# A two-layer encoder on one core: layer 0's attention and output projection issued from an instruction list

## The chip, the cores and the metric

The kernel runs on one core of a Trainium2 chip. A core has a matrix engine (TensorE, PE in the rows; its weight loads are PEld), three engines for elementwise work (VectorE is DVE, ScalarE is ACT, GpSimd is POOL) and a queue engine, SyncE (SP), that issues the loads and stores of weights and activations. Each engine works through its own list of instructions in order and waits at semaphores for the others. The metric is the device time of one execution in microseconds (us); the number quoted for a kernel is the median of several.

## The reference

Two groups of tokens, one prompt of 256 and one sample of 512, each with 16 meta tokens in front, go through the same two layers in fp32. Layer 0 is multi-head latent attention, layer 1 a windowed attention with sinks; each is followed by a squared-ReLU MLP, and each of the four sublayers by a residual and a layer norm. What the change touches is layer 0's attention, cut to its core:

```python
def mla_attend(qn, qr, kn, kr, v):
    s = einsum('bqhd,bkhd->bhqk', qn, kn) + einsum('bqhr,bkr->bhqk', qr, kr)
    p = softmax(s * 96 ** -0.5)
    return einsum('bhqk,bkhd->bqhd', p, v)

c = x @ w_in                                   # 1024 -> 768 + 256 + 32
cq, ckv = rms_norm(c[:768]), rms_norm(c[768:1024])
kr = apply_rope(c[1024:])                      # one for all 16 heads
qn, qr = split(cq @ w_uq)                      # 64 + 32 a head
qr = apply_rope(qr)
kn, v = split(ckv @ w_ukv)                     # 64 + 64 a head
h = layer_norm(4 ** 0.25 * h + mla_attend(...) @ w_o)
```

## The kernel before, in words

There are 800 token columns: `s=0` is the prompt (272), `s=1` the sample (528). Activations lie with features on partitions. Every fp32 product is made of three matmuls in a reduced fp32 form (`mm3`, L440 to L443: high x high, high x low, low x high), so each operand is kept as a high part (a cast on ScalarE) and a low part (a subtraction on VectorE); L458 does both for activations, L314 and L315 for weights.

The stages run one after another: input projection (tile `in`), attention of layer 0, its output projection (tile `o`) with the first half of the layer norm beside it, the MLP, attention of layer 1, the second MLP. For layer 0's attention the 16 heads go in eight pairs `p`, each for `s=0` and then `s=1`. The query columns of a group are cut in chunks of about 100: three for `s=0`, where one chunk does both heads of the pair, five for `s=1`, each head apart. For one chunk (`soft_items`, L737):

- TensorE makes the scores in a PSUM tile `s` (six matmuls; two such tiles exist).
- VectorE takes the row maximum (L766, L773) and scales it; ScalarE takes the exponential into the tile `p`, with its row sums (L768, L776); VectorE inverts these (L769, L777).
- The probabilities are multiplied by the inverse. The 16 meta columns and some more go into a small tile `pk` on VectorE (L743), the 256 or 512 others are scaled in place on GpSimd (L744), for each head.
- TensorE transposes them four blocks at a time (tile `t`, L808) and ScalarE copies the result to `pt` (L814); after all chunks of a unit come the product with the values (`av`, L829) and with the meta values (L837).

Between these steps lies the work that fills TensorE: projections to qn, qr, kn and v for the next pair (`fill_items`, L720). `vmz` and `pks` are small tiles whose unused part must be zero; they are set at L629, in the pool `ap0`, which takes memory that the input's activations `x` held before.

What sets the order here is the framework's scheduler. The code is written in program order, with priorities (`ATT_PRIORITY` for scores and products with the values, 0 for transposes, `LN_PRIORITY` for the layer norm), and the scheduler puts single instructions of each engine into a line by its own estimates. Weights come through the class `Weights`, which loads them in a fixed sequence. `EARLY = 4` of the 16 output tiles are begun for the first column half while the last pair's softmax runs (`early_out`, L901).

Everything later, from the MLP of layer 0 on, is made another way already: by the class `Plan` (L90). There code adds tasks with an engine, an estimated cost, what they read and write, and the buffers they need. TensorE's order is the order in which its tasks are added; the other engines' tasks are placed by a list scheduler (`forward`), which picks by due times worked out backwards and lets buffers rotate in the order in which they are freed; then all instructions are issued in that order, each engine's line as planned.

Of the kernel before, what the change touches and what calls it, by code (L numbers as in the profile page):

```python
# [14 lines left out]
ALU = mybir.AluOpType  # L15
# [44 lines left out]
EARLY = 4  # L60
# [4 lines left out]

SCALE_AHEAD = 3
ATT_PRIORITY, LN_PRIORITY = 30, 300


# [20 lines left out]
class Plan:  # L90
# [8 lines left out]
    def __init__(self, bufs, own):  # L99
        self.bufs, self.own, self.tasks, self.last = bufs, own, [], {}  # L100
        self.given = {tag: [] for tag in bufs}
        self.busy = {}
        self.turns = {tag: [] for tag in bufs}
# [46 lines left out]
    def forward(self, deps, after, late):  # L150
# [13 lines left out]
        def start(i):  # L164
# [3 lines left out]
            for h in held:  # L168
                if id(h) not in at:
                    k = turns[h.tag].index(h)  # L170
                    if len(slots[h.tag]) <= k or k and h.tag not in self.own:
                        return None
                    t = max(t, slots[h.tag][0][0])
# [179 lines left out]
def tile_encoder(ctx: ExitStack, tc: tile.TileContext, ins: dict, y):  # L353
# [31 lines left out]
    def ps_t(name):  # L385
        return bank("t", name)

# [30 lines left out]
    for g in range(4):  # L418
        use(("qr", g), ins["w_qr"][g], 768)
        use(("kv", g), ins["w_kv"][g])  # L420
        use(("qn", 2 * g), ins["w_qn"][2 * g], 768)
        use(("qn", 2 * g + 1), ins["w_qn"][2 * g + 1], 768)
    for hf in range(2):
        for o in range(8):
            use(("o0", hf, o), ins["w_o0"][o])
    for layer in range(2):
        w1 = ins[f"w1_{layer}"]
        if layer == 1:
            for j in UP_FIRST[:2]:
                use(("up", j), None, where="given")  # L430
            for i in range(4):
                use(("dn", 7, i), ins["w2c_1"][i], where="held" if i == 3 else "last")
        else:
            for j in UP_FIRST[:2]:
                use(("up", j), w1[j])
            for i in range(3):
                use(("dn", 7, i), None, where="given")
# [44 lines left out]
    def ln_fm(tp, z, ssum, n, gi, bi, hi, lo, tag, pieces=None, behind=None):  # L482

        pm = ps_l(f"lnm{tag}")
        marks = {"pm": nc.tensor.matmul(pm[:, :n], part, ssum, start=True, stop=True).ins}
        vs = [tp.tile([P, HALF], F32, tag=f"lnv{i}", name=f"lnv{tag}{i}")[:, :n] for i in range(2)]
        for o in range(8):
            f = V.tensor_tensor(z[:, o], z[:, o], pm[:, :n], ALU.subtract)
            if behind is not None:
                after(f.ins, behind["los"][min(7, o + 1)])  # L490
            if o < 2:
                S.activation(vs[o], z[:, o], AF.Square)
            else:
                sq = tp.tile([P, HALF], F32, tag="lnsq", name=f"lnsq{tag}_{o}", bufs=4)
                S.activation(sq[:, :n], z[:, o], AF.Square)
                f = (G if o in POOL_SQUARES and tag != "b0" else V).tensor_tensor(vs[o % 2], vs[o % 2], sq[:, :n], ALU.add)
        marks["va"] = f.ins
        rs = rstd_bcast(tp, vs, n, D, eps_ln, f"ln{tag}", marks)
        for o in range(8):
            f = V.tensor_tensor(z[:, o], z[:, o], rs, ALU.mult)  # L500
            if o >= SCALE_AHEAD:
                after(f.ins, marks["los"][o - SCALE_AHEAD])
            for a, b, d in pieces or [(0, n, 0)]:
                f = S.activation(z[:, o, d : d + b - a], z[:, o, a:b], AF.Identity, bias=gb[:, bi, o : o + 1], scale=gb[:, gi, o : o + 1])
                if o > 0:
                    after(f.ins, marks["hi"])
            marks["hi"], marks["lo"] = split(hi[:, o], lo[:, o], z[:, o, : d + b - a])
            marks.setdefault("los", []).append(marks["lo"])
        return marks


# [6 lines left out]
    acc = hp.tile([P, 2, 8, HALF], F32, tag="acc", name="acc")  # L518
    att = ExitStack()
# [71 lines left out]
    psum_phase(s=2, t=2, w=2)  # L591
# [19 lines left out]
    for s in (1, 0):  # L611
# [4 lines left out]
    def krope(s):  # L616
        for ka, kb in ((272, 400), (400, 800)) if s == 1 else ((0, 272),):
            for e in range(2):
                rows = slice(ROPE[e], ROPE[e] + 32)
                c = slice(ka - 272 * s, kb - 272 * s)  # L620
                split(K[s][e][0][rows, c], K[s][e][1][rows, c], kr[rows, ka // HALF, ka % HALF : (kb - 1) % HALF + 1])

# [3 lines left out]
    vmz = [ap.tile([96, 3, 256], F32, tag=f"vm{i}", name=f"vm{i}") for i in range(2)]  # L626
    pks = [[ap.tile([106, 96], F32, tag=f"pk{i}{e}", name=f"pk{i}{e}") for e in range(2)] for i in range(3)]
    for t in vmz + sum(pks, []):
        G.memset(t, 0.0)  # L629
    wkv, wq, V_ = {}, {}, {}  # L630

    early = []

    def ps_p(name):
        tag = early.pop(0) if early else "w"
        return ps_s(name)[:, 0] if tag == "s" else bank(tag, name)
# [4 lines left out]
    def rope_items(g):  # L641
        def piece(s, a, b):
            if s == 0:
                wq["r"] = W.get(("qr", g), 0)
# [302 lines left out]
    for f in late:  # L947
        f()
# [1279 lines left out]
```

## Time and profile before

| | us |
|---|---|
| median of three runs | 1814.65 (1810.26 to 1816.73) |
| the profiled execution | 1813.73 |
| its span in the trace | 1811.9 |
| PE busy, weight loads | 1769.5, 1635.5 |
| DVE, ACT, POOL busy | 1344.1, 1013.8, 784.9 |

The profiled execution is one run of the program; the span is what lies between its first and last record. The input projection ends at 87.3 us; the first scores come at 100.36, the first early output tile at 381.0, the last product with the values ends at 429.2, and the last output tile at 485.5, where the MLP begins. The mean clock that TensorE was granted is 0.992 of full speed.

### The profile page before, as it was taken

The numbers are of one execution on the slowest core, as the hardware profiler recorded it, in microseconds if no ns is written. First come the engines' busy times: TensorE is split into PE (matmuls) and PEld (weight loads), VectorE is DVE, ScalarE is ACT, GpSimd is POOL, SyncE is SP. The second block draws the span as 40 slices with busy tenths as digits, with TensorE's granted clock in tenths as the row PEclk, the third lists the DMA queues.
The fourth block names the chain that finished last, engine by engine and source line by source line (L and its number), as shares of the span: only waits on it lengthen the run. The fifth ranks groups of instructions, "written<-read, shape, count | busy, mean of one in ns | idle before, by whom it ended". The sixth has DMA issues, their size and how long they took to land.

```text
span 1811.9 us, 28961 instructions
## 1 busy us (share of the span) xinstructions
PE 1769.5 (98%) x10808; PEld 1635.5 (90%) x10808; DVE 1344.1 (74%) x2553; ACT 1013.8 (56%) x2141; POOL 784.9 (43%) x617
## 2 busy tenths in 40 slices
PE   9989999999999999999999899999999999999997
PEld 9989889878999999999999898778989888988995
DVE  5478777775876787787786777876875787778777
ACT  5357766773664456445544536775574456545652
POOL 0046655653244456445533133332233566455623
PEclk9999999999999999999999899999999999999998
DMA  5111001103321121221222222011311221222122
GB/s 196 47 42 31 19 22 34 38 29 125 105 82 47 70 70 47 94 70 47 71 82 89 72 70 68 22 60 59 116 47 59 70 70 49 92 70 70 52 89 93
DMA packets 38444, 121.70 MB, mean 67 GB/s; under 512 B 4640, under 2 KB 9376, under 8 KB 38176
## 3 DMA queue, kind: packets, MB, share of 16 engines
q1 hardware_dynamic: 38304, 119.85, 19.8%
q8 instruction: 85, 1.39, 0.3%
q14 instruction: 55, 0.45, 0.1%
HBM read 116.69 MB, written 3.15 MB: 66 GB/s over the span
## 4 chain that ended last, share of the span: by engine, by line
PE 75%; DVE 16%; ACT 5%; issue 2%; POOL 1%; DMA 1%; DVEq 0%; SPq 0%; ACTq 0%; POOLq 0%
PE w L441 14%; PE w L442 14%; PE w L443 14%; PE wb L441 4%; PE wb L442 4%; PE wb L443 4%; DVE h L1099 2%; DVE wsp0d L1057 2%; PE wb L1904 1%; PE in L441 1%; PE in L442 1%; PE in L443 1%; DVE acc L1364 1%; PE wb L1804 1%; PE wb L1886 1%
## 5 line engine op out<-in xcount | busy, mean ns | idle before, releaser
L744 POOL TENSOR_SCALAR p<-p,rs 106x512 f32<-106x512 f32 (+3 forms) x128 | 184.6, 1451 | 136.4 <-DVE pk L743 66.2
L1364 DVE TENSOR_TENSOR acc<-acc,w 128x400 f32<-128x400 f32 (+1 forms) x306 | 177.0, 617 | 21.3 <-PE w L443 18.9
L1099 DVE TENSOR_TENSOR h<-sq,h 128x384 fp32r<-128x384 f32 (+1 forms) x165 | 139.4, 860 | 23.8 <-ACT h L1097 23.6
L441 PE MATMUL w<-h,wsp0d 128*128 128x400 f32 x336 | 116.1, 346 | 1.1 <-DVE acc L1364 1.1
L442 PE MATMUL w<-h,wsp0d 128*128 128x400 f32 x336 | 116.0, 345 | 0.0
L443 PE MATMUL w<-h,wsp0d 128*128 128x400 f32 x336 | 115.6, 344 | 0.0
L441 PE MATMUL w<-wsp1d,h 128*128 128x512 f32 x252 | 100.1, 397 | 5.6 <-DVE acc L1364 5.6
L1105 POOL TENSOR_TENSOR sq<-sq,sq 128x400 f32<-128x400 f32 (+1 forms) x56 | 74.9, 1338 | 69.6 <-DVE h L1099 60.7
L443 PE MATMUL w<-wsp1d,h 128*128 128x512 f32 x252 | 100.2, 398 | 0.2
L442 PE MATMUL w<-wsp1d,h 128*128 128x512 f32 x252 | 99.9, 396 | 0.0
L1097 ACT CAST h<-sq 128x384 fp32r<-128x384 f32 (+1 forms) x165 | 84.6, 519 | 25.6 <-POOL sq L1105 23.9
L1070 POOL TENSOR_TENSOR wraw0d<-wraw0d,wraw0d 128x512 f32<-128x512 f32 x48 | 69.6, 1468 | 41.2 <-DMA wraw0d<-in_w2b_dram 29.1
L768 ACT ACTIVATE p<-s,nm,rq 106x528 f32<-106x528 f32 (+1 forms) x80 | 63.5, 794 | 42.4 <-DVE nm L767 36.0
L1278 DVE TENSOR_TENSOR sq<-sq,w 128x400 f32<-128x400 f32 (+1 forms) x69 | 38.5, 560 | 56.6 <-PE w L443 56.4
L1051 ACT CAST wsp0d<-wraw0d 128x1024 fp32r<-128x1024 f32 x42 | 43.3, 1051 | 57.7 <-POOL wraw0d L1070 45.9
L766 DVE TENSOR_REDUCE nm<-s 106x1 f32<-106x528 f32 (+1 forms) x80 | 55.8, 700 | 19.9 <-PE s L443 19.0
L1057 DVE TENSOR_TENSOR wsp0d<-wraw0d,wsp0d 128x1024 fp32r<-128x1024 f32 x42 | 63.4, 1510 | 7.0 <-ACT wsp0d L1051 7.0
L1070 POOL TENSOR_TENSOR wraw1d<-wraw1d,wraw1d 128x512 f32<-128x512 f32 x36 | 53.3, 1498 | 31.8 <-DMA wraw1d<-in_w2b_dram 14.4
L315 DVE TENSOR_TENSOR wsp<-wraw,wsp 128x1024 fp32r<-128x1024 f32 (+2 forms) x52 | 55.5, 1076 | 15.1 <-ACT wsp L314 14.8
L441 PE MATMUL s<-k,q 128*106 128x264 f32 (+5 forms) x208 | 62.3, 300 | 4.3 <-ACT p L776 3.2
L441 PEld LDWEIGHTS w<-h,wsp0d 128*128 128x128 f32 x336 | 63.1, 188 | 3.0 <-DVE acc L1364 2.8
L441 PEld LDWEIGHTS w<-wsp1d,h 128*128 128x128 f32 x252 | 47.3, 188 | 18.4 <-ACT wsp1d L1051 8.0
(1444 smaller groups left out, 6409.0 us busy)
## 6 DMA issues: line engine op xcount, KB each, us to landing
wraw0d<-in_w2b_dram SPq DMA_DIRECT2D x24, 512.0 KB, 3.2
wraw1d<-in_w2b_dram SPq DMA_DIRECT2D x18, 512.0 KB, 4.2
wraw<-in_w_o_dram SPq DMA_DIRECT2D x16, 512.0 KB, 3.4
wrawo<-in_w_o_dram SPq DMA_DIRECT2D x16, 512.0 KB, 3.3
wrawq<-in_w_q_dram SPq DMA_DIRECT2D x8, 512.0 KB, 3.3
wraw<-in_w_in_dram SPq DMA_DIRECT2D x6, 512.0 KB, 4.6
wraw<-in_w_qn_dram SPq DMA_DIRECT2D x8, 384.0 KB, 3.0
wx1d<-in_w2b_dram SPq DMA_DIRECT2D x6, 512.0 KB, 3.2
```

Source lines behind the costliest of these rows:

```text
L441: nc.tensor.matmul(out, lh, rh, start=start, stop=False, **kw)
L442: nc.tensor.matmul(out, lh, rl, start=False, stop=False, **kw)
L443: nc.tensor.matmul(out, ll, rh, start=False, stop=stop, **kw)
L744: G.tensor_scalar(pt[:qm, META:T], pt[:qm, META:T], rs[:qm, h : h + 1], None, ALU.mult)
L766: V.tensor_reduce(nm[:qm, 0:1], v, axis=AX.XY, op=ALU.max, negate=True)
L768: S.activation(pt[:qm].rearrange("p (a b) -> p a b", b=264), v, AF.Exp, bias=nm[:qm, 0:1], scale=sc, accum_out=rs[:qm, 0:1])
L1057: lambda: V.tensor_tensor(dst.t[:, 1, dc], src.t[:, sc], dst.t.bitcast(F32)[:, 0, dc], ALU.subtract),
L1070: lambda x=x, y=y, z=z: G.tensor_tensor(x[0].t[:, x[1]], y[0].t[:, y[1]], z[0].t[:, z[1]], op),
L1097: plan.task("ACT", 530, lambda: S.copy(d.t[:, 0], c.t[:, :n]), reads=[c], writes=[(d, "hi")], new=[d])
L1099: "DVE", 570, lambda: V.tensor_tensor(d.t[:, 1], c.t[:, :n], d.t.bitcast(F32)[:, 0], ALU.subtract),
L1105: plan.task("POOL", 185 + 1.67 * n, lambda: G.tensor_tensor(out.t[:, :n], x.t[:, :n], y.t[:, :n], op), reads=[x, y], writes=[out])
L1364: f = lambda: V.tensor_tensor(z, z, ps.t[:, : z.shape[-1]], ALU.add)
```

## The change

Layer 0's attention, its output projection and the half of the layer norm that goes with it become one `Plan` of their own, built by `attention0` and issued with the scheduler's own ordering off. The helpers that layer 1's attention had for itself (new buffers, splits, weight loads, layer norm) move into `steps(plan)`, which both use. The parts:

- The order in which `attention0` adds tasks is TensorE's order: for each chunk the scores, then a waiting step of a product with the values, then the transposes of the chunk that was scored `TRANSPOSE_LAG = 3` chunks before, then fill tasks in proportion.
- PSUM goes from two `s`, two `t` and two `w` tiles (an `s` tile is two banks) to two `s` and four `w`, and transposes and products use `w` too. `nm` and `rs`, the row maxima and sums, have six buffers for four.
- Three early output tiles instead of four.
- The weights of qn, kv, qr, o and the first two of the MLP are loaded and split by tasks of the plan; there are three weight slots, handed from plan to plan.
- The zero-filled tiles lie in a pool `zp` of their own, opened and set at the start of the program.
- Of the scaling in place, the 256-column ones and the first head's 512-column ones go to VectorE; the second head's stay on GpSimd, as a product of two tensors with the inverse sum broadcast along the row.

```diff
-EARLY = 4
+EARLY = 3
+SCALE_DVE = ((0, 0), (0, 1), (1, 1))
...
+    zp = pool("zp", stack=zs)
+    vmz = [zp.tile([96, 3, 256], F32, tag=f"vm{i}", name=f"vm{i}") for i in range(2)]
+    pks = [[zp.tile([106, 96], F32, tag=f"pk{i}{e}", name=f"pk{i}{e}") for e in range(2)] for i in range(3)]
+    for t in vmz + sum(pks, []):
+        G.memset(t, 0.0)
...
-    psum_phase(s=2, t=2, w=2)
+    psum_phase(s=2, w=4)
...
-            V.tensor_scalar(pk[e][:qm, 32 * j : 32 * j + 32], pt[:qm, 0:32], rs[:qm, h : h + 1], None, ALU.mult)
-            G.tensor_scalar(pt[:qm, META:T], pt[:qm, META:T], rs[:qm, h : h + 1], None, ALU.mult)
...
+                if (s, e) in SCALE_DVE:
+                    on, cost = "DVE", 220 + 0.52 * w
+                    f = lambda row=row, r=r: V.tensor_scalar(row()[:, META:T], row()[:, META:T], r(), None, ALU.mult)
+                else:
+                    on, cost = "POOL", POOL(w)
+                    f = lambda row=row, r=r, w=w: G.tensor_tensor(row()[:, META:T], row()[:, META:T], r().to_broadcast([qm, w]), ALU.mult)
+                plan.task(on, cost, f, reads=[rs], writes=[(pt, x)], port=True)
...
+                for i, (f, tr, is_last, lt) in enumerate(seq):
+                    f()
+                    if late:
+                        late.pop(0)()
+                    todo.append((tr, lt if is_last else []))
+                    if len(todo) > lag:
+                        g, more = todo.pop(0)
+                        g()
+                        late.extend(more)
+                    while fill and spent < total * (i + 1) / (len(seq) - AHEAD[s]) - 1:
+                        c, g = fill.pop(0)
+                        spent += c
+                        g()
...
+        osplit(0, 7)
+        for o in range(EARLY):
+            outs[o](range(7, 8))
...
+        with tc.manual_schedule(engines={mybir.EngineType.PE, mybir.EngineType.DVE, mybir.EngineType.Activation, mybir.EngineType.Pool, mybir.EngineType.SP}):
+            plan.issue(after)
```

What stands where, in three places. The first is VectorE's line at the start of the attention; `k` is the key's low part (its rows from `acc` are the rotary part, from `kn` or `wa` the rest), `qsh` and `qy` are steps of the query's rotary part, `rq` the query's scale. Before:

```order
L315 TENSOR_TENSOR wsp_945<-wraw_946,wsp_945 128x768
L580 TENSOR_TENSOR acc<-acc,sq_795 128x400
L458 TENSOR_TENSOR k_823<-acc,k_822 32x272
L458 TENSOR_TENSOR k_825<-acc,k_824 32x272
L458 TENSOR_TENSOR k_827<-acc,k_826 32x128
L458 TENSOR_TENSOR k_829<-acc,k_828 32x128
L458 TENSOR_TENSOR k_827<-acc,k_826 32x400
L458 TENSOR_TENSOR k_829<-acc,k_828 32x400
L458 TENSOR_TENSOR k_823<-kn_883,k_822 64x272
L458 TENSOR_TENSOR k_825<-kn_883,k_824 64x272
```

And the same place after:

```order
L543 TENSOR_TENSOR acc<-acc,sq_814 128x400
L577 TENSOR_TENSOR k_842<-acc,k_841 32x272
L589 TENSOR_TENSOR wsp_622<-wraw_877,wsp_622 128x768
L577 TENSOR_TENSOR k_842<-wa_892,k_841 64x272
L577 TENSOR_TENSOR k_844<-wa_892,k_843 64x272
L577 TENSOR_TENSOR k_844<-acc,k_843 32x272
L736 STREAM_SHUFFLE qsh_967<-wa_864 128x272
L735 TENSOR_TENSOR qy_969<-wa_864,cosq 128x272
```

Two of the six splits of the rotary part now stand ahead of the query's shuffle; before, all six did, and the two steps of `rq`.

The second place is TensorE's line in the first pair, where a query projection (`qn`, after: `wa`) meets the first scores. Before:

```order
L441 MATMUL qn_1086<-cq_95,wsp_945 128x264
L442 MATMUL qn_1086<-cq_96,wsp_945 128x264
L442 MATMUL s_980<-k_825,q_816 92x272
L443 MATMUL s_980<-k_824,q_817 92x272
L442 MATMUL s_1066<-k_825,q_816 90x272
L443 MATMUL s_1066<-k_824,q_817 90x272
L443 MATMUL qn_1086<-cq_95,wsp_945 128x264
L441 MATMUL qn_1086<-cq_95,wsp_945 128x264
```

After, at the first scores of the sample:

```order
L428 MATMUL wa_864<-cq_114,wsp_622 128x264
L426 MATMUL sa_1057<-k_845,q_837 106x264
L427 MATMUL sa_1057<-k_846,q_837 106x264
L428 MATMUL sa_1057<-k_845,q_838 106x264
L426 MATMUL sa_1057<-k_845,q_837 106x264
L427 MATMUL sa_1057<-k_846,q_837 106x264
L428 MATMUL sa_1057<-k_845,q_838 106x264
L945 MATMUL wa_903<-ident,p_1044 128x92 x4
L426 MATMUL wa_881<-wsp_752,ckv_116 128x256
```

Before, matmuls of a projection and of two score tiles alternate; after, each task stands whole.

The third is VectorE's line at a chunk of the prompt. `p` is the tile of probabilities, `rs` their inverse row sums, `pk` the small tile. Before:

```order
L777 RECIPROCAL rs_978<-rs_978 92x2
L743 TENSOR_SCALAR pk_844<-p_979,rs_978 92x32
L743 TENSOR_SCALAR pk_845<-p_979,rs_978 92x32
L458 TENSOR_TENSOR y_841<-qy_1042,y_840 128x264
L666 CAST q_818<-y_840 32x528
```

After:

```order
L900 RECIPROCAL rs_1045<-rs_1045 92x2
L577 TENSOR_TENSOR k_848<-wa_903,k_847 64x264
L905 TENSOR_SCALAR pk_97<-p_1044,rs_1045 92x32
L905 TENSOR_SCALAR pk_98<-p_1044,rs_1045 92x32
L911 TENSOR_SCALAR p_1044<-p_1044,rs_1045 92x256 x2
L577 TENSOR_TENSOR k_848<-wa_881,k_847 64x264
L892 TENSOR_REDUCE nm_1158<-sa_1010 90x2
```

The two scalings of 256 columns, which stood in GpSimd's line, are now in VectorE's, ahead of the next row maximum.

## Rows read from the trace of the kernel before

**Rows 1.** The page: totals; chain; two groups (busy us, mean ns, idle before).
```profile
PE 1769.5 (98%) x10808; PEld 1635.5 (90%) x10808; DVE 1344.1 (74%) x2553; ACT 1013.8 (56%) x2141; POOL 784.9 (43%) x617
...
PE 75%; DVE 16%; ACT 5%; issue 2%; POOL 1%; DMA 1%; DVEq 0%; SPq 0%; ACTq 0%; POOLq 0%
...
L744 POOL TENSOR_SCALAR p<-p,rs 106x512 f32<-106x512 f32 (+3 forms) x128 | 184.6, 1451 | 136.4 <-DVE pk L743 66.2
...
L1070 POOL TENSOR_TENSOR wraw0d<-wraw0d,wraw0d 128x512 f32<-128x512 f32 x48 | 69.6, 1468 | 41.2 <-DMA wraw0d<-in_w2b_dram 29.1
```

**Rows 2.** Table of stretches: PE, PEld, DVE, ACT, POOL busy (instructions), clock, DMA share, GB/s.
```profile
87.30:127.30 40.00, 34.45 (x251) 32.38 (x250) 31.76 (x82) 24.05 (x64) 16.11 (x24) 0.91 0.14 47
127.30:367.30 240.00, 236.55 (x2075) 215.31 (x2074) 181.66 (x539) 169.59 (x454) 145.03 (x101) 1.00 0.09 27
367.30:429.20 61.90, 57.40 (x413) 47.92 (x414) 40.52 (x100) 39.07 (x99) 33.94 (x22) 0.97 0.14 43
429.20:485.50 56.30, 56.25 (x324) 55.54 (x318) 40.48 (x55) 26.84 (x39) 12.10 (x10) 1.00 0.48 154
700.00:900.00 200.00, 199.32 (x1089) 197.68 (x1088) 158.27 (x221) 106.80 (x192) 106.97 (x80) 1.00 0.20 69
1093.00:1250.00 157.00, 155.64 (x1210) 120.25 (x1209) 117.77 (x428) 118.51 (x344) 49.21 (x61) 1.00 0.13 42
87.30:429.20 341.90, 328.40 (x2735) 295.62 (x2735) 253.95 (x720) 232.70 (x616) 195.07 (x146) 0.99 0.10 32
96.40:113.10 16.70, 11.48 (x85) 10.14 (x83) 14.50 (x41) 8.21 (x22) 2.25 (x2) 1.00 0.08 25
113.10:119.90 6.80, 6.61 (x28) 6.16 (x29) 4.72 (x15) 2.38 (x7) 3.07 (x4) 0.50 0.00 0
```

**Rows 3.** Groups of the attention, and the same table for tile o alone.
```profile
L837 PE MATMUL av<-ptm,vm 96*64 96x106 f32 (+4 forms) x254 | 18.0, 254 | 0.0
...
381.00:429.20 48.20, 21.22 (x95) 17.95 (x95) 9.75 (x18) 6.52 (x14) 0.96 0.14 44
```

**Rows 4.** TensorE's instructions: start, duration, engine, line, operation.
```profile
85.68 0.34 PE L441 MATMUL in<-x,wsp 128*128 128x400 f32 x1
87.15 0.35 PE L443 MATMUL in<-x,wsp 128*128 128x400 f32 x1
...
250.26 0.53 PE L808 MATMUL t<-ident,p 106*128 106x106 f32 x4
250.56 0.35 PE L441 MATMUL s<-k,q 96*104 96x264 f32 x1
...
254.72 2.36 PE L829 MATMUL av<-pt,v 128*64 128x318 f32 x16
256.91 0.35 PE L837 MATMUL av<-ptm,vm 96*64 96x106 f32 x2
...
260.32 0.28 PE L442 MATMUL qn<-cq,wsp 128*128 128x264 f32 x1
262.25 0.28 PE L443 MATMUL qn<-cq,wsp 128*128 128x264 f32 x1
```

**Rows 5.** Waits from 87.3 to 429.2: total us, times, longest.
```profile
POOL p L744 <- DVE pk L743: 66.2, 42, 4.9
...
PE s L441 <- ACT p L776: 3.2, 4, 1.6
```

**Rows 6.** The startup's instructions.
```profile
87.37 0.74 POOL L629 MEMSET vm<- 96x768 f32 x1 [85.88 <-PE in L442]
...
91.12 3.42 DVE L458 TENSOR_TENSOR k<-acc,k 32x272 fp32r<-32x272 f32 x6
...
98.06 0.39 PE L441 MATMUL qr<-cq,wsp 128*128 128x264 f32 x1 [1.38 <-DVE qsh L651]
```

**Rows 7.** One line's instructions: duration min/median/max, starts, forms.
```profile
L1857 DVE TENSOR_SCALAR sma<-sma,rs x32: 345/360/1136, 1103.4 to 1189.2; 128x272 f32<-128x272 f32 x32
L1857 DVE TENSOR_SCALAR smb<-smb,rs x16: 417/425/1165, 1194.2 to 1241.4; 128x400 f32<-128x400 f32 x16
```

More of the change, by code (lines that the diff above doesn't have):

```diff
@@ L417, in tile_encoder @@
         use(("in", o), ins["w_in"][o])
[L418 to L425, printed above, removed]
-    for layer in range(2):
[L427 to L437, printed above, removed]
+    use(("qr", 0), ins["w_qr"][0], 768)
+    use(("kv", 0), ins["w_kv"][0])
+    for layer in range(2):
+        for key in [("up", j) for j in UP_FIRST[:2]] + [("dn", 7, i) for i in range(3)]:
+            use(key, None, where="given")
+    use(("dn", 7, 3), ins["w2c_1"][3], where="held")
     W = Weights(nc, wp, specs, 3, 3, 2)
@@ L479, in sq_tile @@
         return pool.tile([P, HALF], F32, tag="sq", name=f"sq{nm}", bufs=6)
[L482 to L509, printed above, removed]
     psum_phase(w=6, l=2)
@@ new lines, in attention0 @@
+        while todo or late:
+            if late:
+                late.pop(0)()
+            if todo:
+                g, more = todo.pop(0)
+                g()
+                late.extend(more)
+            if fill:
+                fill.pop(0)[1]()
+        for _, g in fill:
+            g()
+        osplit(0, 7)
+        for o in range(EARLY):
+            outs[o](range(7, 8))
+        for k in range(8):
+            osplit(1, k)
+        for o in range(EARLY, 8):
+            f = out_steps(0, o)
+            for ks in (range(0, 4), range(4, 8)):
+                f(ks)
@@ new lines, in attention0 @@
+        mean, sums, scale = layer_norm("a0", 0, acc[:, 0], HALF, 0, 1, lambda: a0["ss"], lambda o: (a0["h"][0][:, 0, o], a0["h"][1][:, 0, o]), "h", "sqa", [st2])
+        after0 = {(0, 3): mean, (2, 2): sums, (3, 0): scale}
+        for o in range(8):
+            f = out_steps(1, o)
+            for i in range(4):
+                f(range(2 * i, 2 * i + 2))
+                if (o, i) in after0:
+                    after0[o, i]()
+        ahead = [t.weights(ins["w1_0"][j], f"up{j}") for j in UP_FIRST[:2]]
@@ L989, in tile_encoder @@
+        for x in ahead:
+            x.left += 1
+        with tc.manual_schedule(engines={mybir.EngineType.PE, mybir.EngineType.DVE, mybir.EngineType.Activation, mybir.EngineType.Pool, mybir.EngineType.SP}):
+            plan.issue(after)
+        for j, x in zip(UP_FIRST, ahead):
+            W.give(("up", j), x.t)
+    attention0()
     wo.close()
+    zs.close()
+    h, sqp, late_sum = a0["h"], a0["sqp"], a0["late"]
     def h2_tile(mp, nm, n):
@@ L1016, in weights @@
         def weights(nm):
[L1017 removed]
+            return new("wsp")
         def raw(src, nm, tag="wraw"):
@@ L1591, in attention1 @@
         plan.busy = {"DVE": 700.0, "ACT": 700.0, "POOL": 300.0}
-        DVE, ACT, POOL = lambda n: 150 + 1.05 * n, lambda n: 170 + 0.835 * n, lambda n: 185 + 1.67 * n
-        MM = {400: 183, 384: 174, 256: 119}
-        both = lambda *names: [(x, y) for x in names for y in ("hi", "lo")]
+        t = steps(plan)
+        new, split_to, weights, layer_norm = t.new, t.split_to, t.weights, t.layer_norm
         st1 = plan.stage("projections", open_projections)
@@ L2011, in some @@
             while done < upto and not (through and n < 12 + behind):
-                cost, f = next(steps)
+                cost, f = next(beside)
                 done += cost
@@ L2033, in attention1 @@
                 outputs(*ITEMS[n - behind], *turned.pop(n - behind))
-        for _, f in steps:
+        for _, f in beside:
             f()
```

834 lines of the change are left out of this document (448 added, 386 removed).

## Prediction

> **What bounds the kernel now.** I read the page's totals and its chain first, then a table of stretches, the waits in the stretch that the change touches, and TensorE's single instructions there. The reader is to see in the totals that TensorE is busy 98% of the span and carries 75% of the chain that ended last [rows 1], so only TensorE's order and the waits in it can move the time. The change touches TensorE's work from the end of the input projection (87.3 us) to the first MLP matmul (485.5 us): what the other engines run from there on stands in the same order in both kernels. In that table the attention is the first three stretches, 341.90 us together, and the rest of the output projection the fourth, 56.30 us [rows 2]. The last is already dense (PE busy 56.25, weight loads 55.54). In the attention PE is busy 328.40 and its weight loads 295.62, so idle time is 13.50: 5.55 in the first 40 us, 3.45 in the next 240, 4.50 in the last 62.
>
> Busy time hides more. A 264-column matmul is shown with 0.28 us though the next starts after about 0.12 [rows 4]: a wait shorter than the difference leaves no gap. So I count the work by pitch, the distance from one start to the next. In [rows 4]: 264 columns, 16 steps from 260.32 to 262.25, 0.1206 each; 400 columns, 8 steps from 85.68 to 87.15, 0.184; four transposes 0.30 (250.26 to 250.56); 16 rows of a 318-column product with the values 2.19 (254.72 to 256.91), 0.137 each. With the counts from the loops: scores 480 x 0.1206 + 144 x 0.124 (272 columns by their share) = 76; qn 432, qr 216, kn 144 matmuls = 52.9 + 26.4 + 17.6; v 168 x 0.117 (0.1206 by 256 of 264 columns) = 19.6; 104 groups of transposes x 0.30 = 31.2; products with the values, 320 rows by width, 36.6, and with the meta values 18.0 [rows 3]; the small rest some 6. That is 284. Before also does 95 of the 96 matmuls of its 4 early output tiles here (the count is in [rows 3]): 95 x 0.184 = 17.5. So 301 us of work take 341.9: 40 are lost. Of these 13.5 are idle, 5.3 are half clock (6.80 us at 0.50 of full speed, the 1.2 GHz level, half of which counts as loss, with PE busy 6.61 in them and, in the 16.70 us ahead, 11.48; and 0.97 of 61.90 in the last stretch, 1.9 [rows 2]), and about 22 are hidden in busy time.
>
> Beside that row stands a rule. The Trainium skill, "Perfetto Trace Analysis", section "Identifying the Most-Contended Engine", calls matmul busy share a bad measure for TensorE because matmuls are pipelined, and names the weight-load share. The trace agrees: 96% busy and 86% weight load here, and 99.7% and 98.8% in 200 us of the planned MLP [rows 2]. By busy share alone 13.5 us could be won, less the 5.9 of the early tiles below, and the sum would end near 1807; by the pitch 40 could.
>
> **The change part by part.**
>
> *TensorE's order.* Before, Tile's scheduler mixes work matmul by matmul; after, one score group runs as six in a row, then a group of transposes, then a piece of projection. What is gained are losses, not work. The upper end of what may be left is all 40 (the new order waits as much). The lower end is read from planned stretches of the same kernel: 157 us of the second layer's attention have 1.36 idle, 0.9%, and 200 us of MLP have weight loads 98.8% busy [rows 2]; 0.9% + 1.2% of 318 is 7. Between them I take 22.5: idle 6.5, half clock 1, hidden 15. The startup keeps 3 idle, since its chain (rotary, casts, splits, first score) is data; the tail keeps 2 around the last softmax. The hidden part keeps two thirds: each score group still waits for a bank of two, freed by the exponential on ScalarE, as the longest PE wait of before does (3.2 us in 4 waits [rows 5]). That is nearer to the middle than to the planned rows, because these have wider products per handoff.
>
> *Startup.* Before, the second qr product waits 1.38 us for VectorE's shuffle, which stood behind six splits of k (3.42 us) [rows 6]; after, two of the six stand ahead of it and four later, and the products rotate over four banks. The 1.38 goes; late next is the first score, on the q and k splits. It is within the 3 that I keep.
>
> *Zero tiles.* The eight memsets lay on x, so the first waited 85.88 us for TensorE and then took 0.74 [rows 6]. In a place of their own they run at the start, where POOL waits for data anyway; the q and k zero casts come some 2 us sooner. PE's largest waits are on ScalarE and VectorE [rows 5, 6], not on these: worth 0, at most 1 either way.
>
> *Early tiles.* 4 become 3, each with 7 of its 8 steps written ahead of the last product with the values: 63 matmuls stand there instead of 95. Attention's work becomes 284 + 3 x 21 x 0.184 = 295.6; with 22.5 of losses T = 318. The stretch behind it gets 95 - 63 = 32 matmuls more, 32 x 0.184 = 5.9 on 56.30, so 62.2. The tie between output work and layer norm is as in the second layer's plan; its bounds are 4 and 9 us, by a tile of 24 more or less filled in.
>
> *Scaling.* 128 POOL scalings (184.6 us, mean 1451 ns [rows 1]) become 88 on VectorE (40 of 512 columns, 48 of 256) and 40 on POOL as tensor by broadcast. No row shows VectorE scaling these; nearest is a scaling of 272 and 400 columns, medians 360 and 425 ns, up to 1136 and 1165 [rows 7]. That is 0.51 ns a column: 0.482 for 512 and 0.352 for 256, so 19.3 + 16.9 = 36.2 us alone; at the longest, 1.15 each, 101. On POOL a tensor operation of 512 columns took 1.468 [rows 1]: 40 are 59, against 184.6. VectorE's own operations should lose some of the time that they now spend beside POOL; I take 8. VectorE goes from 253.95 to about 282 of 318, 89%; the planned MLP has it at 158.27 of 200.00, 79% [rows 2]. It gains that the transposes wait for a 0.5 us scaling, not for one of 1.45 behind a POOL queue (POOL waited 66.2 us for the pk scaling [rows 5], so this queue was not full; that is why the gain isn't larger). Each scaling queues the next max and q or k splits behind it by 0.35 to 0.48.
>
> *More buffers* (nm and rs 6 for 4) and the weights' loads by the plan: the same 254 SP issues, DMA busy 9 to 14% in the attention [rows 2]; 0.
>
> Sum from the profiled execution, 1813.73 us (span 1811.9): 1813.73 - 341.9 + 318 + 5.9 = 1795.7. The median of before, 1814.65, is 0.9 above that execution, so **1797**.
>
> **The rivals.** Each is 1813.73 - 341.9 + 5.9 + 0.9 = 1478.6, plus its T.
> A, the forecast: 0.52, own range 1786 to 1806 (losses 12 to 32).
> B, the hidden stalls stay: only idle and clock improve, losses 33, T 328.5: 1807. For it: the number of handoffs is the same. Against: whole groups of six matmuls (0.72 us) hide a handoff better than single ones. 0.16.
> C, nearly as dense as the MLP: losses 9, T 305: 1784. For it: 0.9% idle in the second layer. Against: two score banks. 0.06.
> D, VectorE becomes the bound. Place: the steady 240 us, VectorE's queue between a score's max and its pk scaling. If it cannot be kept busier than the 79% of that MLP stretch, T = 282 / 0.79 = 357: 1836, slower. It decides from a share of 282 / 336 = 0.84, where T + 5.9 is 341.9. For it: no planned stretch in [rows 2] has VectorE busier (158.27 of 200.00 and 117.77 of 157.00). Against: there it waits for TensorE, it isn't the bound. 0.09.
> F, VectorE and POOL exclude each other: one scaling takes 345 ns or 1136 [rows 7], as if it had stood behind a whole POOL operation. If none of their work overlapped, T could not be under 282 + 59 = 341, the time 1820, slower; it decides from a sum of 336. Against it: before has 253.95 + 195.07 = 449 us of both in 341.90 [rows 2], so much overlaps. 0.05. The Trainium skill, "SBUF — State Buffer", section "SBUF: two separate sides", calls the port pair that VectorE and GpSimd share an exclusive lock, held for a whole instruction, the loser fully blocked. By that rule the long scalings are expected, and the 449 us say that it cannot hold for all instructions here.
> E, gains are lost again (tail, early tiles, startup), T about 337: 1816, no change. For it: the output projection is dense already, so every tile taken from the attention is paid there. 0.12.
>
> **How the numbers follow.** About 0.3% (5 us) is what a measurement of this kernel tells from no change. A and C and most of B (all but 0.02, its upper edge) are faster: 0.72. That 0.02 and 0.10 of E are the same: 0.12. D, F and the 0.02 of E that overshoots are slower: 0.16. The range holds 8 of 10: from 1781, a little under C, to 1818, over E and short of F and D, with the bounds of the losses and of the early tiles within it.
>
> **What would show it.** Attention from the last input matmul to the last product with the values: 318 (right), over 336 (D, E or F). Its PE idle 6 to 7 us and weight loads over 91% busy; no half-clock stretch after the first scores. VectorE busy 275 to 290 in it; scaling rows of 0.35 to 0.6 us mean. If the mean is near 1.1 us and TensorE's waits end on VectorE's scaling, D holds. If the stretch behind takes over 66 us, E does. Wrong would be the whole working if time moved behind 485.5 of before, in the MLP or the second layer.

## The result, and the profile after

The changed kernel takes 1798.19 us (median of four, 1797.57 to 1799.5) against 1812.88 of the kernel before measured beside it: a ratio of 0.9918, 95% interval 0.9897 to 0.9939. Forecast were 1797 us and a gain. Its profiled execution took 1798.46 us, the span 1796.4.

One correction first. The description of the change ahead has the two heads the wrong way round: by the table `((0, 0), (0, 1), (1, 1))` it is the second head's 512-column scalings that go to VectorE, and the first head's that stay on GpSimd. The counts are the same.

The page of the changed kernel, its totals and the engines of its chain; they answer to [rows 1]. Line numbers are the changed kernel's; in the rows of another run they are that run's own:

```profile
PE 1757.5 (98%) x10808; PEld 1626.9 (91%) x10808; DVE 1363.0 (76%) x2641; ACT 1017.1 (57%) x2141; POOL 639.1 (36%) x529
...
PE 79%; DVE 11%; ACT 4%; issue 3%; POOL 2%; DMA 1%; SPq 0%; DVEq 0%; ACTq 0%; POOLq 0%
```

Its table of stretches (columns as in [rows 2]), cut where the input projection ends, in the first 40 us, the middle, the tail, the rest of the output projection, the whole attention, and the stretch in which the kernel before starved:

```profile
87.56:127.56 40.00, 37.35 (x312) 35.22 (x312) 35.55 (x102) 28.97 (x77) 6.78 (x13) 1.00 0.13 40
127.56:360.00 232.44, 227.90 (x2020) 207.49 (x2020) 199.81 (x603) 172.01 (x450) 34.05 (x32) 1.00 0.09 29
360.00:408.32 48.32, 45.44 (x377) 39.54 (x374) 34.76 (x99) 34.53 (x89) 6.25 (x6) 1.00 0.09 27
408.32:471.90 63.58, 62.20 (x350) 61.06 (x348) 47.56 (x65) 30.35 (x44) 17.08 (x13) 1.00 0.51 163
87.56:408.32 320.76, 310.69 (x2704) 282.25 (x2704) 270.12 (x802) 235.50 (x613) 47.08 (x50) 1.00 0.10 30
96.40:113.10 16.70, 16.20 (x132) 15.69 (x130) 15.64 (x49) 12.08 (x32) 0.00 (x0) 1.00 0.01 1
```

The attention, T in the forecast, is 320.76 us for 341.90. The clock is 1.00 in all of it: 96.40 to 113.10 is busy 16.20 us where before had 11.48, and the stretch at 0.50 that followed is gone. The idle time is 10.07 (37.35 of 40.00 and so on) for 13.50. By the pitches of the forecast, with the matmuls counted stretch by stretch, the losses are 26 us for 41 (40 in the forecast's sum): about 4 for 11 in the first 40 us, 6 for 13 in the last stretch (48 us for 62), but in the 232 to 240 us between still 16 for 18. The gain is at the two ends.

Behind it the output projection is 63.58 us for 56.30, and the first 13 us of the MLP lose a wait of before (1.65 us for the last row sum; its row in before is below), so that every matmul behind it starts another 1.9 us earlier. From 500.5 us of before on, every matmul stands 14.5 to 15.9 us earlier. So the gain is 21.14 - 7.28 + 1.88, less 0.26 by which the input projection ended later: 15.5, the difference of the spans.

```profile
488.40 0.91 PE L1140 MATMUL w<-sqsum,part 128*128 128x400 f32 x2 [1.65 <-DVE sqsum L985]
```

VectorE's and GpSimd's scaling in the changed kernel, each line's instructions (duration min/median/max, first and last start, forms); they answer to the row of L744 in [rows 1] and to [rows 7]:

```profile
L911 DVE TENSOR_SCALAR p<-p,rs x88: 340/350/491, 109.3 to 401.4; 90x256 f32<-90x256 f32 x32, 106x512 f32<-106x512 f32 x32, 92x256 f32<-92x256 f32 x16, 104x512 f32<-104x512 f32 x8
L914 POOL TENSOR_TENSOR p<-p,rs x40: 1040/1042/1329, 119.7 to 398.8; 106x512 f32<-106x512 f32 x32, 104x512 f32<-104x512 f32 x8
```

### The profile page after: what moved, and what is told of

It reads as the page before. It is cut to its first block, busy times and chain, and to the rows that moved or that the text cites. A ratio compares the mean times of both kernels' runs of the same rounds, so it can differ in the third digit from the quotient of the medians.

```text
span 1796.4 us, 28830 instructions
## 1 busy us (share of the span) xinstructions
PE 1757.5 (98%) x10808; PEld 1626.9 (91%) x10808; DVE 1363.0 (76%) x2641; ACT 1017.1 (57%) x2141; POOL 639.1 (36%) x529
## 4 chain that ended last, share of the span: by engine, by line
PE 79%; DVE 11%; ACT 4%; issue 3%; POOL 2%; DMA 1%; SPq 0%; DVEq 0%; ACTq 0%; POOLq 0%
PE w L426 14%; PE w L427 13%; PE w L428 13%; PE wb L426 4%; PE wb L427 4%; PE wb L428 4%; DVE wsp L1245 3%; PE wa L426 2%; PE wa L428 2%; PE wa L427 2%; PE wa L978 2%; DVE h L1287 2%; PE sa L426 2%; PE wb L2018 1%; PE in L427 1%
## 5 line engine op out<-in xcount | busy, mean ns | idle before, releaser
L426 PE MATMUL w<-h,wsp 128*128 128x400 f32 x632 | 218.3, 345 | 1.8 <-DVE acc L1552 1.1
L427 PE MATMUL w<-h,wsp 128*128 128x400 f32 x632 | 218.3, 345 | 0.0
L428 PE MATMUL w<-h,wsp 128*128 128x400 f32 x632 | 217.5, 344 | 0.1
L1552 DVE TENSOR_TENSOR acc<-acc,w 128x400 f32<-128x400 f32 (+1 forms) x306 | 176.8, 615 | 21.9 <-PE w L428 19.6
L914 POOL TENSOR_TENSOR p<-p,rs 106x512 f32<-106x512 f32 (+1 forms) x40 | 42.6, 1066 | 264.9 <-ACT pt L953 77.5
L426 PE MATMUL w<-wsp,h 128*128 128x512 f32 x300 | 119.4, 398 | 5.5 <-DVE acc L1552 5.5
L426 PEld LDWEIGHTS w<-h,wsp 128*128 128x128 f32 x632 | 118.8, 188 | 4.4 <-DVE acc L1552 3.0
L428 PEld LDWEIGHTS w<-h,wsp 128*128 128x128 f32 x632 | 118.7, 188 | 1.0 <-DVE wsp L1245 0.7
L428 PE MATMUL w<-wsp,h 128*128 128x512 f32 x300 | 119.2, 397 | 0.4
L427 PEld LDWEIGHTS w<-h,wsp 128*128 128x128 f32 x632 | 118.6, 188 | 0.9 <-DVE h L1287 0.5
L427 PE MATMUL w<-wsp,h 128*128 128x512 f32 x300 | 118.9, 396 | 0.0
L428 PE MATMUL w<-t,wsp 128*128 128x400 f32 (+1 forms) x336 | 114.5, 341 | 0.0
L427 PE MATMUL w<-t,wsp 128*128 128x400 f32 (+1 forms) x336 | 114.1, 340 | 0.0
L426 PE MATMUL w<-t,wsp 128*128 128x400 f32 (+1 forms) x336 | 114.0, 339 | 0.0
L1258 POOL TENSOR_TENSOR wraw0d<-wraw0d,wraw0d 128x512 f32<-128x512 f32 x48 | 69.2, 1461 | 42.8 <-DMA wraw0d<-in_w2b_dram 29.5
L427 PE MATMUL w<-hc,wsp 128*128 128x384 f32 x232 | 78.8, 340 | 0.5 <-DVE hc L1372 0.3
L426 PE MATMUL w<-hc,wsp 128*128 128x384 f32 x232 | 79.2, 341 | 0.1
L428 PE MATMUL w<-hc,wsp 128*128 128x384 f32 x232 | 78.4, 338 | 0.0
```

The costliest lines, as they stand in the source:

```text
L426: nc.tensor.matmul(out, lh, rh, start=start, stop=False, **kw)
L427: nc.tensor.matmul(out, lh, rl, start=False, stop=False, **kw)
L428: nc.tensor.matmul(out, ll, rh, start=False, stop=stop, **kw)
L914: f = lambda row=row, r=r, w=w: G.tensor_tensor(row()[:, META:T], row()[:, META:T], r().to_broadcast([qm, w]), ALU.mult)
L1258: lambda x=x, y=y, z=z: G.tensor_tensor(x[0].t[:, x[1]], y[0].t[:, y[1]], z[0].t[:, z[1]], op),
L1552: f = lambda: V.tensor_tensor(z, z, ps.t[:, : z.shape[-1]], ALU.add)
```

## The experiments

Each run is one kernel; "T" is its attention in the profiled execution, from the first matmul behind the input projection to the first behind the last product with the values, "out" what follows up to the MLP (so before's T is 342.08 here, 341.90 in [rows 2]). Early output matmuls within T are 95 in the kernels made from before, 42 with two early tiles, 63 in all others, so T and out are to be read together. "Written" stands for the whole plan: TensorE's order as written, the other engines' as the plan places them, and the weights' loads; no run has TensorE's order alone.

| run | order | PSUM | other parts | T | out | median us | ratio to before, 95% |
|---|---|---|---|---|---|---|---|
| before | scheduler | 2 t + 2 w | none | 342.08 | 56.09 | | 1 |
| changed | written | 4 w | all | 320.76 | 63.58 | 1798.19 | 0.9918 (0.9897 to 0.9939) |
| order_only | written | 2 t + 2 w | none | 338.51 | 62.61 | 1813.5 | 1.0006 (0.9995 to 1.0018) |
| order_w4 | written | 4 w | none | 324.01 | 62.61 | 1799.47 | 0.9923 (0.9908 to 0.9938) |
| psum_t | written | 2 t + 2 w | all | 335.40 | 63.08 | 1814.44 | 1.0000 (0.9991 to 1.0010) |
| before_w4 | scheduler | 4 w | none | 368.10 | 56.09 | 1839.12 | 1.0141 (1.0126 to 1.0156) |
| pool_scale | written | 4 w | all but VectorE's scaling | 322.21 | 62.62 | 1797.84 | 0.9916 (0.9900 to 0.9932) |
| pool_ts | written | 4 w | same, GpSimd in before's form | 324.10 | 62.62 | 1798.33 | 0.9919 (0.9904 to 0.9934) |
| zero_back | written | 4 w | all but the zero tiles' place | 320.51 | 63.54 | 1797.62 | 0.9914 (0.9898 to 0.9930) |
| before_scale | scheduler | 2 t + 2 w | VectorE's scaling | 353.89 | 56.09 | 1824.84 | 1.0064 (1.0045 to 1.0084) |
| psum_t_mixed | written, k q k q | 2 t + 2 w | all, early tiles off t | 321.20 | 62.62 | 1800.84 | 0.9926 (0.9912 to 0.9941) |
| w3 | written | 3 w | all | 333.57 | 63.53 | 1813.95 | 0.9998 (0.9988 to 1.0007) |
| mixed | written, k q k q | 4 w | all | 322.95 | 63.53 | 1800.3 | 0.9923 (0.9908 to 0.9938) |
| early2 | written | 4 w | all, 2 early tiles | 315.80 | 65.40 | 1795.05 | 0.9894 (0.9878 to 0.9911) |

**First set: is it the order, the scaling or the zero tiles?**

order_only undoes every part of the changed kernel but the written order and the three early tiles:

```diff
-SCALE_DVE = ((0, 0), (0, 1), (1, 1))
+SCALE_DVE = ()
-psum_phase(s=2, w=4)
+psum_phase(s=2, t=2, w=2)
-            f = lambda row=row, r=r, w=w: G.tensor_tensor(row()[:, META:T], row()[:, META:T], r().to_broadcast([qm, w]), ALU.mult)
+            f = lambda row=row, r=r: G.tensor_scalar(row()[:, META:T], row()[:, META:T], r(), None, ALU.mult)
...
-        ps = new("s" if o % 3 == 2 else "w")
+        ps = new("wts"[o % 3])
```

Transposes and products with the values take t, nm and rs have four buffers, and the zero tiles lie in `ap0` again.

> The changed kernel with every other part undone: all scaling on GpSimd as a scaling by a column, zero tiles in the input's place, two t and two w tiles of PSUM, four nm and rs; only three early tiles remain, since four need a fourth weight slot. Theory 1 (TensorE's order at the two ends of the attention gives the gain): at least 10 of the 15 us stay, 1798 to 1804, the startup's losses stay near 5 us and the half-clock stretch after the first scores stays away. Rival 2 (the scaling on VectorE gives it): 1807 or more. Rival 3 (the zero tiles give it): 1805 or more, with the losses in the first 40 us.

pool_scale has one edit:

```diff
-SCALE_DVE = ((0, 0), (0, 1), (1, 1))
+SCALE_DVE = ()
```

> The changed kernel with all 128 scalings on GpSimd, as products with a broadcast. 128 x about 1.05 us for 512 columns and half for 256 is some 110 us on GpSimd of 320. Theory 1: 1798 to 1802, TensorE's waits at the transposes grow by 1 to 3 us, VectorE gives back about 36 us. Rival 2: 1805 or more, the loss spread over the steady 232 us. A loss of VectorE's crowding (the forecast's D in small): 1795 or less.

zero_back has only the zero tiles taken from `ap0` again:

```diff
-    vmz = [zp.tile([96, 3, 256], F32, tag=f"vm{i}", name=f"vm{i}") for i in range(2)]
...
+    vmz = [ap.tile([96, 3, 256], F32, tag=f"vm{i}", name=f"vm{i}") for i in range(2)]
...
```

> The changed kernel with the zero tiles back in the memory of the input's activations, so the memsets wait for the input projection. Theory 1: 1798 to 1800, nobody waits for them. Rival 3: 1802 or more, the loss in the first 40 us of the attention, with waits that end on GpSimd.

before_scale is the kernel before with the scaling alone:

```diff
-            G.tensor_scalar(pt[:qm, META:T], pt[:qm, META:T], rs[:qm, h : h + 1], None, ALU.mult)
+            if T == 272 or e == 1:
+                V.tensor_scalar(pt[:qm, META:T], pt[:qm, META:T], rs[:qm, h : h + 1], None, ALU.mult)
+            else:
+                G.tensor_tensor(pt[:qm, META:T], pt[:qm, META:T], rs[:qm, h : h + 1].to_broadcast([qm, T - META]), ALU.mult)
```

> The kernel before with one part alone: the 256-column scalings and the second head's 512-column ones on VectorE, the first head's on GpSimd as a product with a broadcast. Theory 1: within 5 us of before either way, 1808 to 1820, since the losses at both ends don't hang on it. Rival 2: 1805 or less.

All three theories fell. The written order alone gains nothing (1.0006); the scaling and the zero tiles can be taken back without loss. The scaling alone, under the scheduler, even costs 0.6%: 1824.84 us, outside the 1808 to 1820 that theory 1 had expected. What order_only had kept from before, beside scaling and zero tiles, were the PSUM split, the four nm and rs and GpSimd's form of the scaling. Its waits of TensorE in the attention (engine, line, waited for: total us, times, longest) show which to try first:

```profile
PE wa L426 <- DVE k L572: 8.1, 8, 1.0
PE sa L426 <- ACT p L888: 3.4, 10, 0.4
PE ta L946 <- POOL p L915: 2.7, 3, 1.9
```

`wa` is a projection, `k` a VectorE split that empties a projection's PSUM tile. No such wait stands in the changed kernel, whose largest are these two:

```profile
PE sa L426 <- ACT p L887: 4.3, 12, 0.5
PE wa L426 <- ACT p L897: 1.3, 1, 1.3
```

**Second set: the banks, or the form of GpSimd's operation?**

psum_t is the changed kernel with before's tiles; transposes and products with the values take t:

```diff
-    psum_phase(s=2, w=4)
+    psum_phase(s=2, t=2, w=2)
...
-        ps = new("s" if o % 3 == 2 else "w")
+        ps = new("wts"[o % 3])
```

> The changed kernel with before's PSUM split: two tiles t for transposes and products with the values, two tiles w for projections, instead of four w for all. Theory 4, formed on the run with the order alone (where projections waited 8.1 us in 8 waits for VectorE's splits of k, that is for a bank): the four rotating banks give most of the gain, 1808 or more, with those waits back. Rival 5 (the form of GpSimd's operation gives it: the scaling by a column took 1457 ns on average, the product with a broadcast 945): 1798 to 1803.

order_w4 is order_only with the changed kernel's tiles:

```diff
-    psum_phase(s=2, t=2, w=2)
+    psum_phase(s=2, w=4)
...
```

> The run with the order alone, but with four w tiles: all scaling on GpSimd by a column, zero tiles in the input's place, four nm and rs. Theory 4: 1797 to 1803. Rival 5: 1807 or more.

pool_ts is pool_scale with GpSimd's operation in before's form:

```diff
-f = lambda row=row, r=r, w=w: G.tensor_tensor(row()[:, META:T], row()[:, META:T], r().to_broadcast([qm, w]), ALU.mult)
+f = lambda row=row, r=r: G.tensor_scalar(row()[:, META:T], row()[:, META:T], r(), None, ALU.mult)
```

> The changed kernel with all 128 scalings on GpSimd in before's form, by a column. Theory 4: 1797 to 1802, a few us of waits at the transposes. Rival 5: 1807 or more, GpSimd busy some 185 us again and the transposes waiting for it.

before_w4 is the kernel before with

```diff
-        return bank("t", name)
+        return bank("w", name)
...
-    psum_phase(s=2, t=2, w=2)
+    psum_phase(s=2, w=4)
...
-    early += ["t", "t", "s", "s", "w", "w"]
+    early += ["w", "w", "s", "s", "w", "w"]
```

> The kernel before with one part alone: four w tiles in PSUM for transposes, projections and products with the values, under the scheduler's order. If the banks alone give the gain: 1803 or less. If they need the written order, since the scheduler interleaves projections matmul by matmul and holds their banks longer: 1808 to 1820.

The four corners are now measured, with T in us: scheduler and 2 + 2 tiles 342.08, scheduler and 4 tiles 368.10, written order and 2 + 2 tiles 338.51, written order and 4 tiles 324.01. Neither edit gains alone. The 3.6 us that the order takes off T stand behind it again (out 62.61 for 56.09), and the banks alone cost 26 us of T, far outside both ranges expected for before_w4. Together they give the whole effect, with scaling, zero tiles and buffers left as before (order_w4, 0.9923). The form of GpSimd's operation decides nothing (pool_ts, 0.9919). Rival 5 fell, theory 4 stood.

psum_t also shows where two tiles fail. The instructions at one of the nine places (start, duration, engine, line, operation; in brackets the wait): two k projections of six matmuls each in a row, the casts and splits that empty their tiles, and the q projection behind them:

```profile
142.87 0.37 PE L426 MATMUL wa<-ckv,wsp 128*128 128x264 f32 x1
...
143.88 1.54 ACT L575 CAST k<-wa 64x264 fp32r<-64x264 f32 x4 [0.64 <-PE wa L428]
...
144.28 0.28 PE L428 MATMUL wa<-ckv,wsp 128*128 128x264 f32 x1
144.67 1.78 DVE L577 TENSOR_TENSOR k<-wa,k 64x264 fp32r<-64x264 f32 x4 [0.72 <-ACT k L575]
...
145.60 0.40 PE L426 MATMUL wa<-cq,wsp 128*128 128x264 f32 x1 [1.04 <-DVE k L577]
```

The first k projection fills one w tile in 0.72 us, the second the other; the third in the row needs the first tile, which two casts and two splits of about 0.4 us each are still emptying. The wait is 1.03 to 1.04 us in seven of the nine places, 0.87 and 0.15 in the two of the startup. The Trainium skill, "Perfetto Trace Analysis", section "Optimization Strategy", reads such a gap, repeating on the engine that should be saturated, as a sign that there may not be enough SBUF or PSUM for the next tile. This trace agrees: 9 waits, 8.3 us, at the longest 1.0.

**Third set: why two tiles fail, and what is left to win.**

psum_t_mixed is psum_t with two edits:

```diff
-(T2, lambda: knope(1, p, 0)), (T2, lambda: knope(1, p, 1)), (T6, lambda: qnope(1, p, 0)), (T6, lambda: qnope(1, p, 1))]
+(T2, lambda: knope(1, p, 0)), (T6, lambda: qnope(1, p, 0)), (T2, lambda: knope(1, p, 1)), (T6, lambda: qnope(1, p, 1))]
...
-        ps = new("wts"[o % 3])
+        ps = new("s" if o % 3 == 2 else "w" if o < EARLY and hf == 0 else "wt"[o % 3])
```

> The run with two t and two w, with two edits that give two w tiles room: the four projections of a prompt step are written k, q, k, q instead of k, k, q, q, so that a q projection no longer needs the tile that the first k projection filled 0.7 us before; and the early output tiles lie in w, w, s as in the changed kernel instead of w, t, s, so that transposes keep both t. Theory 4a (two w tiles fail at these two places, the third projection in a row and the tail): the 8.3 us of waits for VectorE's splits fall under 2, the losses in the last 40 us from 13 to 6 or 8, 1800 to 1806. Theory 4b (transposes and products need more than two tiles everywhere): 1810 or more.

w3 is the changed kernel with one bank unused:

```diff
-    psum_phase(s=2, w=4)
+    psum_phase(s=2, w=3)
...
```

> The changed kernel with three w tiles, one bank of PSUM left unused. Theory 4a: a third tile covers the third projection in a row, so most of the gain stays, 1799 to 1806. Theory 4b: transposes, products and projections crowd on three, 1810 or more.

early2 is the changed kernel with

```diff
-EARLY = 3
+EARLY = 2
```

> The changed kernel with two early output tiles. By the forecast's term 21 matmuls x 0.184 = 3.9 us move behind the attention; if the last softmax has no other work to hide it, as much is lost, 1800 to 1803; if the tail's 5.6 us of losses don't hang on the early work: 1797 to 1799.

mixed is the changed kernel with the first edit of psum_t_mixed.

> The changed kernel with the four projections of a prompt step written k, q, k, q and nothing else changed. With four tiles no wait of TensorE there is on VectorE's splits, so 1796 to 1799 by theory 4a; faster than 1795 only if hidden waits of under 0.16 us stood there.

Two w and two t are enough once the order suits them: psum_t_mixed is at 0.9926. So the gain does not need four shared tiles, only an order that fits the tiles there are. Here theory 4a, that two w tiles fail at two places only, stood. Its largest wait on a split is this one; the 8.3 us are gone:

```profile
PE sa L426 <- ACT p L888: 4.1, 11, 0.5
...
PE wa L426 <- DVE q L577: 0.3, 1, 0.3
```

psum_t's table of stretches, first 40 us, middle and tail:

```profile
89.10:129.10 40.00, 36.43 (x290) 34.18 (x289) 32.69 (x95) 27.37 (x72) 6.53 (x12) 0.96 0.12 37
129.10:360.00 230.90, 221.60 (x1966) 201.73 (x1965) 191.45 (x585) 165.15 (x434) 32.29 (x30) 1.00 0.10 30
360.00:424.50 64.50, 57.77 (x453) 48.99 (x451) 43.16 (x123) 42.52 (x109) 9.32 (x8) 0.96 0.06 21
```

The same of psum_t_mixed:

```profile
89.50:129.50 40.00, 36.98 (x292) 34.47 (x291) 33.05 (x95) 27.48 (x73) 6.54 (x12) 0.96 0.12 37
129.50:360.00 230.50, 227.78 (x2020) 208.03 (x2019) 195.71 (x600) 170.39 (x446) 33.31 (x32) 1.00 0.10 30
360.00:410.70 50.70, 48.48 (x398) 41.53 (x396) 38.26 (x109) 37.03 (x95) 6.45 (x7) 1.00 0.08 26
```

The k q k q order takes the waits out of the middle, where no output tile runs yet: idle 9.30 becomes 2.72. In the tail, where both edits act and no run parts them, idle 6.73 becomes 2.22, and the granted clock comes back from 0.96 to 1.00 of full speed. Of psum_t's 14.6 us against the changed kernel, idle makes 19.6 - 10.1 = 9.5, and the clock, as an estimate from these rows, 0.04 x 40 + 0.04 x 64.5 = 4.2.

w3 missed what theory 4a expected: three tiles for all are as bad (0.9998) as two and two. Its table:

```profile
87.55:127.55 40.00, 37.54 (x310) 35.16 (x310) 34.93 (x100) 28.56 (x76) 6.68 (x12) 1.00 0.12 38
127.55:360.00 232.45, 223.86 (x1971) 202.56 (x1970) 193.52 (x589) 166.06 (x437) 33.71 (x31) 1.00 0.09 29
360.00:421.12 61.12, 54.45 (x428) 45.69 (x426) 39.77 (x115) 40.07 (x102) 7.64 (x7) 0.97 0.07 22
```

The first 40 us are as in the changed kernel; idle is lost in the middle (8.59 for 4.54) and the tail (6.67 for 2.88), in many waits of at most 1.1 us at scores, transposes and projections. There theory 4b fits, that they crowd on one shared pool of three; no further run tested it. How many tiles are needed thus depends on which work shares them: two for projections and two for transposes do with an order that spaces the projections, three for both do not with the order as written.

early2 is faster than the kernel before, 1795.05 us, 0.9894, but its interval overlaps that of the changed kernel: a gain over that one is not shown. Its profiled execution was the slowest of its four, 1798.03 us, with an input projection that ended 2.2 us later than the changed kernel's. In its trace T and out:

```profile
89.80:405.60 315.80, 306.66 (x2684) 278.63 (x2683) 270.03 (x802) 234.98 (x613) 47.32 (x50) 1.00 0.10 31
405.60:471.00 65.40, 65.40 (x370) 65.09 (x369) 48.67 (x63) 30.34 (x43) 16.06 (x13) 1.00 0.48 152
```

T loses 5.0 us, of which 3.9 are the 21 matmuls moved; out gets only 1.8 longer, mostly since the 1.4 us that TensorE idled there (62.20 of 63.58) are gone. The expectation had a loss or nothing, 1797 at the least. mixed, at four tiles, brought nothing (0.9923, T 2.2 us longer), a little over the 1796 to 1799 expected.

## Why the prediction was right, step by step

The time, its sign and the size of the largest term were right: T 320.8 for 318, out 63.6 for 62.2, sum 1795.7 for the execution's 1798.46. In part this was luck: the errors of 2.8 and 1.4 met 1.9 us won in the MLP, where the forecast had said that nothing would move, and the banks, without which the order gains nothing, were in the change though the sum had no term for them. So the reason given was only half of one. Of its signs, T, the clock, the scaling's duration and the stretch behind (63.6, under 66) held; the idle time (10.1 us for 6 to 7), the weight loads (282.25 of 320.76, 88%, for over 91%) and VectorE (270 us for 275 to 290) lay outside.

*TensorE's order.* The forecast put the gain on the written order, with four banks named in half a sentence on the startup. The runs showed that this order gives nothing on the banks of before (order_only, 1.0006), while one with the k and q projections in turn and the early tiles off t does, beside the scaling and zero tiles of the changed kernel (psum_t_mixed, 0.9926). In the changed kernel the losses fell by the order and the banks together: this step failed in its mechanism, though not in its size (losses 26 for 22.5). What would have shown it: the written order puts whole projections behind each other, and a look at what empties each one's tile, two casts and two splits, against two tiles. The Trainium skill, "Perfetto Trace Analysis", section "Matmuls", says that independent matmul groups should rotate through different PSUM banks, so that emptying one overlaps the next group. It bore on this case more than either rule that the forecast weighed, and the corners agree with it, for the written order alone: under the scheduler four shared tiles cost 26 us of T.

*Hidden losses.* Taken as 22 before and 15 after, spread over the attention. The size was right: of the 26 us left, 10 are idle and none is half clock, so 16 are hidden. Their place was not: the middle lost 18 by pitch and still loses 16, of which 4.5 are idle. Some 10 more, an estimate from the starts in the trace, are no wait that the profile names: in both traces, where TensorE goes from one kind of product to another (scores to products with the values, these to the meta products, these to transposes), a start comes about 0.1 us later than the pitch. Here the product with the values starts 0.21 us behind the last score matmul, where the pitch of the scores is 0.12:

```profile
196.87 0.28 PE L427 MATMUL sa<-k,q 96*106 96x264 f32 x1
196.99 0.28 PE L428 MATMUL sa<-k,q 96*106 96x264 f32 x1
197.20 1.14 PE L978 MATMUL wa<-pt,v 128*64 128x272 f32 x8
```

This part was mis-named as waiting: both orders have these changes, and whether one with fewer of them gains was not tried. The gain came from the ends instead, by idle time, half clock and hidden losses there.

*Startup.* Right: the wait for the shuffle went, the idle kept was 2.65 for the forecast's 3, and with it the half clock (0.91 to 1.00). It comes back, 0.93, in order_only.

*Tail.* Idle kept 2.9 for 2, no half clock. The early tiles cost 7.3 us behind for 5.9; the price was known, but early2, with one early tile fewer, gives no sign that the third is worth it.

*Zero tiles.* Worth 0 as forecast: 0.9914 with them back.

*Scaling.* The price was right on VectorE, 34.2 us for 36.2 (340 to 491 ns a scaling); on GpSimd the 40 products took 42.6 us for 59. VectorE is busy 270.1 us for 282, since its other work lost 18 us (270.1 - 34.2 for 253.95) where the forecast took 8. Its worth was not right: taking it back costs T 1.5 us (pool_scale), in before's form 3.3 (pool_ts), and neither shows in the time. The scaling was hardly on TensorE's path here: TensorE's listed waits for it sum to 1.5 us.

*The rivals.* D fell: VectorE runs at 84% of T, its own break-even, and 89% of the first 40 us, and TensorE's listed waits on it in T sum to 0.5 us. F fell as a bound, by pool_ts, where VectorE (243.5) and GpSimd (182.4) together have 426 us in 324. As a mechanism between single instructions it is there in the changed kernel, though the scalings do not show it: the plan places GpSimd's work and VectorE's tasks marked `port=True`, the scalings among them, one after the other by its estimates, and none of VectorE's 88 lies beside one of GpSimd's 40. The query's casts are not marked. Nine of them took 1.11 to 1.27 us, each beside a GpSimd product, and the other 55 took 0.27 to 0.43. The first row is all of them, the others are one such pair:

```profile
L747 DVE CAST q<-y x64: 270/417/1273, 99.0 to 363.9; 32x272 fp32r<-32x272 f32 x32, 32x528 fp32r<-32x528 f32 x32
...
211.88 1.04 POOL L914 TENSOR_TENSOR p<-p,rs 104x512 f32<-104x512 f32 x1 [3.75 <-DVE nm L893]
211.94 1.27 DVE L747 CAST q<-y 32x528 fp32r<-32x528 f32 x1
```

B was right for the middle alone, but its sum does not follow from its words: with idle 6.5, half clock 1 and 22 hidden the losses are 29.5 and not 33, the time 1804. In the same way all idle time won would end near 1801 and not 1807, since the early tiles' 5.9 us only move. C and E did not come.

What stays open: why four shared tiles cost the scheduler's order 26 us of T, and why VectorE's scaling costs it 12. Both traces show more idle time in T (21.3 and 21.2 us for 13.5) and a lower granted clock (0.97 for 0.99). In the first 40 us TensorE is busy about as long as before (33.5 and 34.9 us for 34.5), at a clock of 0.87 for 0.91; most of the loss lies later. The longest waits of before_w4 are those of scores for the exponential (7.4 us in 6); what makes these late was not tried.

## What to carry to other kernels

A written order and the buffers that it runs on are one edit: price them together, by asking of each task in a row which buffer it needs and what is still emptying it. When several parts change at once, measure the corners, since parts that gain nothing alone (here the order, 1.0006, and the banks, 1.0141) may be the whole gain together (0.9923). Read losses stage by stage: here what could be won lay at both ends, and most of what is lost in the middle stayed, some 10 of 16 us as steps between kinds of product and not as waits. An order that keeps two engines' tasks apart can hide that they hold each other up: look also at the tasks that it does not keep apart.

## What was not expected of the hardware

GpSimd's product of two tensors with a broadcast was faster than its scaling by a column, but beside it VectorE was slower. These are the groups of GpSimd's scaling and of one VectorE cast beside it (busy us, mean ns, idle before). In pool_ts:

```profile
L914 POOL TENSOR_SCALAR p<-p,rs 106x512 f32<-106x512 f32 (+3 forms) x128 | 177.9, 1399 | 136.1 <-DVE pk L905 91.6 <-DVE rs L890 28.9 <-DVE nm L884 3.8
...
L747 DVE CAST q<-y 32x272 fp32r<-32x272 f32 (+1 forms) x64 | 28.2, 455 | 1.2
```

In pool_scale:

```profile
L914 POOL TENSOR_TENSOR p<-p,rs 106x512 f32<-106x512 f32 (+3 forms) x128 | 119.7, 945 | 191.9 <-DVE pk L905 116.6 <-DVE rs L890 39.8 <-DVE nm L884 5.9
...
L747 DVE CAST q<-y 32x272 fp32r<-32x272 f32 (+1 forms) x64 | 31.9, 514 | 1.2
```

GpSimd is 58 us less busy in the second, and VectorE 13 us more, for the same work (256.8 for 243.5 in T). The kernel's time is the same in both, 1797.84 and 1798.33 us.
